# Three pairs of a scan's output products as seven block products among the next projections, decay factors on ScalarE

## Chip, cores and metric

One core of a Trainium2 chip runs the whole program. The metric is the device time of one execution in microseconds; of the kernel before three runs were timed: 2537.12 in the median, 2536.92 to 2539.6.

## What is computed

Two pre-norm layers on 256 tokens of width 2048: a Mamba-2 scan and an MLP, then dilated attention and an MLP, and a final norm. The change lies in the scan layer. Cut to what matters:

```python
zxbcdt = u @ w_in                      # z, xbc and dt side by side
xbc = silu(causal_depthwise_conv(xbc, conv_w, conv_b))
...
L = segsum_exp(a)                      # exp(cs[l] - cs[s]) for s <= l, else 0
cb = jnp.einsum("bclgn,bcsgn->bcgls", cm, bm)
y_diag = jnp.einsum("bcgls,bgjcls,bcsgjp->bclgjp", cb, L, x)
...
y = ssd_chunked(xs * dt[..., None], dt * A, bm, cm)
y = y + d_skip[:, None] * xs
y = y.reshape(Bsz, S, D_INNER) * silu(z)
yg = y.reshape(Bsz, S, SSM_GROUPS, D_INNER // SSM_GROUPS)
yg = yg * rsqrt(mean(yg * yg) + EPS)
x = x + (yg.reshape(Bsz, S, D_INNER) * norm_w) @ w_out
```

There are 8 groups of 512 channels (8 heads of 64), 2 chunks of 128 tokens, and a state of 128. All is float32.

## The kernel before, in words

**Matmuls.** Each float32 product is made of rounded parts: a weight is split into a high part `wh` (a ScalarE copy to fp32r, L232) and a low part `wl` (VectorE, the raw weight less `wh`, L233), the activation likewise, and TensorE adds high x high, high x low and low x high. A weight comes in units of 128x2048 (1 MB). `fetch` (L189 to L235) loads one (SyncE's queue, L216) into a raw buffer and splits it; `take` (L237) is called when a unit's matmuls are written down, and fetches every later unit of `plan` whose split buffer belongs to a unit already used. There are three pairs of split buffers (a fourth in the middle of the MLP), so the split of a unit may begin when the unit three places earlier has been multiplied.

**A group of the scan** (`group`, L514) has 10 units of `w_in`: six feature units c0 to c5 (`cols_units`, 16 matmuls of 512 columns and 16 of 256, L260), each followed by a convolution (`conv_tile`, L487: the two halves of a bank added, a scale, four taps, a silu), and four gate units z0 to z3 (`rows_unit`, 24 matmuls of 512 columns, L295 to L297). Then three parts follow, each written where an earlier group's generator is resumed:

- first part: the rows of cumulated decay come by DMA into `ab` (L560, one buffer, which the group before frees with its y matmuls); the product `cb` of the two state features (L574); 16 VectorE steps per group, `min(row - column, 0)` (L585); two Exp on ScalarE (L588); the product with `cb` (L590, "es"); transposes of the features (L597) and their scaled copies `xdt`, `xd`, `xdd`.
- second part: the state `st`, 64 small matmuls `y` (L623), the share of the earlier chunk `yo`, the gate, the norm.
- third part: transposes `yT` (L649) and the high and low parts `y3t` of the result (L655, L656).

**The output product** (`project`, L661) is written in blocks: after group 3 for groups 0 and 1, after group 5 for 2 and 3, after group 7 for 4 and 5, then 6, then 7. Each group has 4 units of `w_out`, one for each 512 columns of the result, 24 matmuls each; two results per unit are added into `x_res` (L302). With group 7 the norm of the next layer starts (`step_on`).

**What sets the order.** A scheduler orders all instructions by the order in which they are written and by their readiness; engines then run their queues strictly in that order and wait for each other by semaphores. `tc.issue_after(i)` keeps an instruction behind another. In the MLP the second product is already made from seven block products (Winograd's form of Strassen): `CHUNK_ORDER` writes feature units U and products in turn, TensorE's order is fixed, and the sums of weight blocks are made in a buffer A and a buffer B, partly by GpSimd's accumulating DMA (L218), which adds one more block onto a buffer after the split before has read it.

Of the kernel before, what the change touches and what calls it, by code (L numbers as in the profile page):

```python
# [14 lines left out]
P = 128  # L15
S = 256
# [28 lines left out]

def unit_plan():
    plan = []
    pairs = {3: (0, 1), 5: (2, 3)}
    for g in range(G):
        plan += [("in", g, u) for u in range(6)]  # L50
        if g == 0:
            plan.append(("dt",))
        plan += [("in", g, u) for u in range(6, 10)]
        if g in pairs:
            plan += [("out", gg, j) for j in range(4) for gg in pairs[g]]
    for gs in ((4, 5), (6,), (7,)):
        plan += [("out", gg, j) for j in range(4) for gg in gs]
# [17 lines left out]
}  # L75

# [16 lines left out]
def hybrid_trunk_kernel(ctx: ExitStack, tc: tile.TileContext, a: dict, out: bass.AP):  # L93
# [58 lines left out]
    def source(u):  # L152
# [32 lines left out]

    def split_slot(i):
        return splits.peek(range(4 if chunked(i) else 3))

    def fetch(i, ends=(16,)):  # L189

        src, n = source(plan[i])
        item = plan[i][3] if plan[i][0] == "w2" and len(plan[i]) == 4 else None
        where, _, _, how = PRODUCTS[item[0]] if item else ("raw", 0, 0, "load")
        if where == "raw":
            k = raws.use(raws.peek(range(2 if chunked(i) else 3)))
            raw = wts.tile([P, 2048], F32, tag=f"raw{k}", name=f"raw{i}", bufs=1)
        elif how == "load":
            if where + item[1] == "Aa":
                pool, tag = wts, f"raw{raws.use(2)}"
            else:  # L200
                pool, tag = mlp_pool[0], where + item[1]
            raw = pool.tile([P, 2048], F32, tag=tag, name=f"{where}{item[1]}{i}", bufs=1)
        else:
            raw = sums_of[where + item[1]]
        if where != "raw":
            sums_of[where + item[1]] = raw
# [6 lines left out]
        for k0, k1 in zip((0, *ends), ends):  # L213
# [3 lines left out]
            elif how == "add":  # L217
                nc.gpsimd.dma_start(raw[:, c], src[:, c], accum_op=ALU.add)  # L218
            with ExitStack() as order:
                if plan[i][0] in ("w1", "w2"):  # L220
# [151 lines left out]
    def ssm(nx):  # L372
# [9 lines left out]
        for j in range(4):  # L382
            n = KT if j == 0 else 0
            t = sp.tile([P, n + (8 if j else 4) * S], F32, tag="y3t", name=f"xt0_{j}", bufs=4)
            if j == 0:
                g0 = t[:, :KT]
            t_x = t[:, n:n + 4 * S].rearrange("p (q t) -> p q t", q=4)
            xt.append((t[:, n:n + 4 * S], t[:, 4 * S:] if j else None))
# [37 lines left out]
        def steps():  # L426
# [56 lines left out]
            sm.update(dt=dt, acs=acs, scratch=scratch, ddt=dec, eacs=eacs)  # L483

        y3 = {}

        def conv_tile(g, u, ps, tot=None):  # L487
# [12 lines left out]
            nc.scalar.activation(o, acc, AF.Silu, bias=cw[:, 4:5])  # L500
# [8 lines left out]
        def cross(ps, lhs, rhs):  # L509
            nc.tensor.matmul(ps, lhs[:, 0], rhs[:, 0], start=True, stop=False)  # L510
            nc.tensor.matmul(ps, lhs[:, 0], rhs[:, 1], start=False, stop=False)
            nc.tensor.matmul(ps, lhs[:, 1], rhs[:, 0], start=False, stop=True)

        def group(g, before):  # L514
# [3 lines left out]
            us, names = [("in", g, u) for u in range(6)], [f"c{g}_{u}" for u in range(6)]  # L518
            if g == 0:
# [17 lines left out]
            else:  # L537
                ch = []
                for u in range(6):
                    ch.append(conv_tile(g, u, cols_units([us[u]], xs, [names[u]], first=(u < 2))[0]))  # L540
                    if u == (4 if g == 1 else 2):
                        next(before, None)
            banks = [mm_bank(f"z{g}_{m}") for m in range(NH)]
            for q in range(4):
                rows_unit(banks, [("in", g, 6 + q)], lhs_x, 4 * q, 4, 512, q == 0, q == 3)
                if q == (3 if g == 1 else 1) and before is not None:
                    next(before, None)
            if g == 0:
                with tc.issue_after(load[12]):
                    for m in range(NH):  # L550
                        nc.sync.dma_start(x_res[:, m, :], a["x"][m * P:(m + 1) * P, :])
            zs = []
            for m in range(NH):
                z = sp.tile([P, GW], F32, tag="z", name=f"zs{g}_{m}", bufs=2)
                nc.scalar.activation(z, banks[m], AF.Silu, scale=n0.rs[:, m:m + 1])
                zs.append(z)

            ab = sp.tile([P, NH, HG, P], F32, tag="ab", name=f"ab{g}", bufs=1)
            rows = sm["scratch"][:, g * HG * P:(g + 1) * HG * P]
            nc.scalar.dma_start(ab.rearrange("p m h t -> p m (h t)"),  # L560
                                rows.unsqueeze(0).to_broadcast([P, NH, HG * P]))
            hs = slice(g * HG, (g + 1) * HG)
            bT, cT = ch[4], ch[5]

            def bc(v):
                return v.unsqueeze(2).to_broadcast([P, HG, HD])

            def heads(t):
                return t.rearrange("p (h d) -> p h d", h=HG)

            ps = sm_bank(f"cb{g}")
            for m in range(NH):
                t = slice(m * P, (m + 1) * P)
                nc.tensor.matmul(ps[:, t], bT[:, t], cT[:, t], start=(m == 0), stop=True,  # L574
                                 skip_group_check=True)
            cb = sp.tile([P, NH, P], F32, tag="cb", name=f"cbm{g}", bufs=1)
            nc.vector.tensor_tensor(cb, ps[:, :S].rearrange("p (m l) -> p m l", m=NH),
                                    tri[:, None, :].to_broadcast([P, NH, P]), ALU.mult)

            es = []  # L580
            for m in range(NH):
                e = ab[:, m]
                for h in range(HG):
                    av = sm["acs"][:, m, g * HG + h:g * HG + h + 1]
                    nc.vector.tensor_scalar(e[:, h], e[:, h], av, 0.0, ALU.subtract, ALU.min)  # L585
                es.append(e)
            for m in range(NH):
                nc.scalar.activation(es[m], es[m], AF.Exp)  # L588
            for m in range(NH):
                nc.vector.tensor_tensor(es[m], es[m], cb[:, m:m + 1, :].to_broadcast([P, HG, P]),  # L590
                                        ALU.mult)

            xdt, xd = [], []
            for m in range(NH):
                ps = sm_bank(f"xt{g}_{m}")
                for c in range(4):
                    nc.tensor.transpose(ps[:, c * P:(c + 1) * P], ch[c][:, m * P:(m + 1) * P], ident)  # L597
                t = sp.tile([P, GW], F32, tag="xdt", name=f"xdt{g}_{m}", bufs=2)
                nc.vector.tensor_tensor(heads(t), heads(ps), bc(sm["dt"][:, m, hs]), ALU.mult)
                xdt.append(t)  # L600
                t = sp.tile([P, GW], F32, tag="xd", name=f"xd{g}_{m}", bufs=2)
                nc.vector.tensor_tensor(heads(t), heads(ps), bc(dskip[:, hs]), ALU.mult)
                xd.append(t)
                if m == 0:
                    t = sp.tile([P, GW], F32, tag="yo", name=f"xdd{g}", bufs=1)
                    nc.vector.tensor_tensor(heads(t), heads(ps), bc(sm["ddt"][:, hs]), ALU.mult)
                    xdd = split(t, GW, "xdd", f"xdds{g}")
            ps = sm_bank(f"bt{g}")
            nc.tensor.transpose(ps[:, :P], bT[:, :P], ident)
            btok = split(ps[:, :P], P, "bs", f"btok{g}")  # L610
            cs = split(cT[:, P:], P, "bs", f"cs{g}")
            yield

            ps = sm_bank(f"st{g}")
            cross(ps, btok, xdd)
            state = split(ps, GW, "xdd", f"state{g}")
            ys = []
            for m in range(NH):
                ps = sm_bank(f"y{g}_{m}")
                for h in range(HG):  # L620
                    for c in range(2):
                        l = slice(c * 64, (c + 1) * 64)
                        nc.tensor.matmul(ps[l, h * HD:(h + 1) * HD], es[m][:, h, l],  # L623
                                         xdt[m][:, h * HD:(h + 1) * HD], start=(h == 0), stop=True,
                                         skip_group_check=True)
                y = xd[m]
# [498 lines left out]
```

## Time and profile before

| | |
|---|---|
| profiled execution | 2538.28 us |
| its span, first to last instruction | 2536.4 us |
| median of three timed runs | 2537.12 us |
| granted TensorE clock | 0.999 |
| busy in the span: TensorE, VectorE, ScalarE, GpSimd | 100%, 80%, 60%, 4% |
| first matmul of the first MLP | 686.65 us |
| matmuls of the scan's output product | 768, of 512 columns |
| read from HBM | 544.16 MB |

A row of a view has line, engine, operation, output and inputs by their names in the program, sizes and a count. In the grouped view, behind the bar, stand the busy time, the mean of one in ns, and the idle time of the engine just before, with what ended it. In the chain and in the timeline a row begins with its start in us from the span's start and its length. The lengths of TensorE and VectorE instructions overlap with the next ones, so the time that one takes in a queue is the distance of two starts.

### The profile page before, as it was taken

Reading aid. Unit: us, or ns where it says so; the run is one execution under the profiler, and the core shown is the slowest. Engines: PE = TensorE matmul, PEld = TensorE weight load, DVE = VectorE, ACT = ScalarE, POOL = GpSimd, SP = SyncE. Lnnn points to the kernel's source line nnn. Section 1 sums busy time; section 2 is a strip of 40 time slices with the busy share of each in tenths; the row PEclk is TensorE's granted clock in tenths of the full one; section 3 lists DMA queues with packets and bytes.
Section 4 is the critical chain, followed back from the end, with each engine's and each line's share of the span. In section 5 each row is a group of like instructions: output and inputs, shape, how many; then the busy total and the mean of one; then the engine's idle time right before and its main releaser. Section 6 shows DMA issues by size and latency. Waiting matters only on the chain.

```text
span 2536.4 us, 34422 instructions
## 1 busy us (share of the span) xinstructions
PE 2523.8 (100%) x13809; PEld 2175.5 (86%) x13809; DVE 2021.8 (80%) x2370; ACT 1532.3 (60%) x1826; POOL 101.0 (4%) x119
## 2 busy tenths in 40 slices
PE   9999999999999999999999999999999999999998
PEld 7888888888888888888888999999888888888887
DVE  7888687687678889888886667767668998889885
ACT  7676466564566666566555656666566666666664
POOL 0000000000000000000000000000000000000001
PEclk9999999999999999999999999999999999999999
DMA  7655555555688898889955545444568988898884
GB/s 283 222 183 194 186 186 193 190 184 183 217 226 247 254 252 260 256 251 254 261 193 175 174 174 169 165 162 163 173 223 231 265 251 252 247 269 252 254 234 143
DMA packets 81105, 548.57 MB, mean 216 GB/s; under 512 B 9008, under 2 KB 9648, under 8 KB 19760
## 3 DMA queue, kind: packets, MB, share of 16 engines
q1 hardware_dynamic: 66096, 447.79, 49.6%
q0 software_dynamic: 12096, 88.09, 17.7%
q10 hardware_dynamic: 2752, 10.49, 1.3%
q8 instruction: 109, 1.79, 0.3%
q14 instruction: 52, 0.43, 0.0%
HBM read 544.16 MB, written 2.16 MB: 215 GB/s over the span
## 4 chain that ended last, share of the span: by engine, by line
PE 98%; DMA 1%; DVE 0%; issue 0%; ACT 0%; SPq 0%; ACTq 0%; POOLq 0%; POOL 0%; DVEq 0%
PE h L260 28%; PE qk L260 11%; PE c L260 10%; PE pxb L938 6%; PE pxa L938 6%; PE pwb L938 3%; PE pwa L938 3%; PE wo L296 2%; PE wo L295 2%; PE z L296 2%; PE z L297 2%; PE z L295 2%; PE wo L297 2%; PE v L297 2%; PE v L295 2%; PE v L296 2%
## 5 line engine op out<-in xcount | busy, mean ns | idle before, releaser
L233 DVE TENSOR_TENSOR wl<-raw,wh 128x2048 fp32r<-128x2048 f32 (+4 forms) x386 | 837.6, 2172 | 336.1 <-ACT wh L232 335.0
L232 ACT ACTIVATE wh<-raw 128x2048 fp32r<-128x2048 f32 (+4 forms) x386 | 704.1, 1826 | 450.5 <-PE wo L297 84.0
L260 PE MATMUL h<-xn,wh 128*128 128x512 f32 x2048 | 690.0, 393 | 0.0
L260 PE MATMUL h<-xn,wl 128*128 128x256 f32 x2048 | 555.5, 280 | 0.0
L260 PEld LDWEIGHTS h<-xn,wh 128*128 128x128 f32 x2048 | 376.4, 188 | 75.8
L260 PEld LDWEIGHTS h<-xn,wl 128*128 128x128 f32 x2048 | 385.0, 188 | 13.8
L260 PE MATMUL c<-xn,wh 128*128 128x512 f32 x768 | 267.5, 395 | 2.2 <-ACT wh L232 2.2
L260 PE MATMUL qk<-xn,wh 128*128 128x512 f32 x768 | 259.3, 393 | 0.0
L260 PE MATMUL c<-xn,wl 128*128 128x256 f32 x768 | 212.4, 282 | 0.8 <-DVE wl L233 0.8
L260 PE MATMUL qk<-xn,wl 128*128 128x256 f32 x768 | 209.2, 283 | 0.0
L260 PEld LDWEIGHTS c<-xn,wh 128*128 128x128 f32 x768 | 143.1, 188 | 35.0 <-ACT wh L232 4.5
L260 PEld LDWEIGHTS qk<-xn,wh 128*128 128x128 f32 x768 | 141.1, 188 | 28.8
L260 PEld LDWEIGHTS c<-xn,wl 128*128 128x128 f32 x768 | 143.7, 188 | 3.6 <-DVE wl L233 1.4
L260 PEld LDWEIGHTS qk<-xn,wl 128*128 128x128 f32 x768 | 141.4, 188 | 3.6 <-issue 1.2
L232 ACT ACTIVATE wh<-Ab 128x2048 fp32r<-128x2048 f32 x42 | 80.4, 1915 | 78.5 <-DMA Ab<-in_w 59.3
L233 DVE TENSOR_TENSOR wl<-Ab,wh 128x2048 fp32r<-128x2048 f32 x42 | 96.0, 2287 | 18.0 <-ACT wh L232 18.0
L232 ACT ACTIVATE wh<-Aa 128x2048 fp32r<-128x2048 f32 x42 | 80.3, 1912 | 40.4 <-DMA Aa<-in_w 33.3
L233 DVE TENSOR_TENSOR wl<-Aa,wh 128x2048 fp32r<-128x2048 f32 x42 | 96.0, 2286 | 9.8 <-ACT wh L232 9.8
L297 PE MATMUL z<-wh,xn 128*128 128x512 f32 x256 | 100.3, 392 | 0.0
L295 PE MATMUL wo<-wh,y3t 128*128 128x512 f32 x256 | 100.2, 393 | 0.0
L296 PE MATMUL wo<-wl,y3t 128*128 128x512 f32 x256 | 100.0, 391 | 0.0
L295 PE MATMUL z<-wh,xn 128*128 128x512 f32 x256 | 100.0, 391 | 0.0
(372 smaller groups left out, 4776.0 us busy)
## 6 DMA issues: line engine op xcount, KB each, us to landing
raw<-in_w SPq DMA_DIRECT2D x172, 1024.0 KB, 5.4
raw<-in_w_in SPq DMA_DIRECT2D x74, 1024.0 KB, 4.9
raw<-in_w_qk SPq DMA_DIRECT2D x48, 1024.0 KB, 4.8
raw<-in_w_out SPq DMA_DIRECT2D x32, 1024.0 KB, 4.8
Aa<-in_w POOLq DMA_DIRECT2D x28, 1024.0 KB, 10.1
Ab<-in_w POOLq DMA_DIRECT2D x28, 1024.0 KB, 10.1
raw<-in_w_v SPq DMA_DIRECT2D x32, 768.0 KB, 4.3
Ab<-in_w SPq DMA_DIRECT2D x14, 1024.0 KB, 4.8
```

The costliest lines, as they stand in the source:

```text
L232: high[i] = nc.scalar.activation(wh[:, c], raw[:, c], AF.Copy).ins
L233: low[i] = nc.vector.tensor_tensor(wl[:, c], raw[:, c], wh[:, c].bitcast(F32), ALU.subtract).ins
L260: latest[0] = nc.tensor.matmul(ps[:, :n], (wh, wl)[part][:, kt * P:(kt + 1) * P], xs[:, kt, :, :].rearrange("p a t -> p (a t)")[:, :n], st ...
L295: nc.tensor.matmul(banks[m][:, :n], hi, wh[:, c], start=st, stop=False)
L296: nc.tensor.matmul(banks[m][:, :n], hi, wl[:, c], start=False, stop=False)
L297: latest[0] = nc.tensor.matmul(banks[m][:, :n], lo, wh[:, c], start=False, stop=sp).ins
L938: latest[0] = nc.tensor.matmul(ps, lhs(i, part), w[:, n], start=(first and i == 0 and part == 0 and w is wh), stop=(i == 3 and part == 1), ...
```

## The change

`GROUP_ORDER` now writes, for each group from 1 on, what is put down in which order: c0 to c5 and z0 to z3 of this group, `y` and `Y` (second part of the group before, in two halves), `t` (its third part), `f` (first part of this group), `p` (operands of a pair), digits (products of the pair in work), `oGJ` (unit J of group G, as before). From group 3 on TensorE's order is fixed to it. The pairs are groups 0 and 1, 2 and 3, 4 and 5; a pair's products for the first half of the columns lie in one group (3, 5, 7), for the second half in the next (4, 6, and the tail 8). Groups 6 and 7 keep plain units, in the tail. Each product has 12 matmuls of 512 columns.

The weight sums of a half are made on buffer A (1: load, 5, 6, 4: one block more added each time) and B (3: load, 7: one more added), all additions by GpSimd's DMA; 2 is a plain load. Two raw buffers are left beside A. The operands of a pair, four sums and seven splits, are 11 steps on VectorE and 7 on ScalarE, put down at `p`. Each product is added into `x_res` by a VectorE step (14 per pair, where 8 were).

The decay factors become `exp(-|row - column|)`: 16 Abs per group on ScalarE with the negated column as bias, then two Exp with scale -1, kept behind the last silus; the upper triangle is masked by `cb` as before.

```diff
+GROUP_ORDER = {
...
+    **{g: "c0 c1 1 c2 y c3 Y 5 c4 3 c5 t 6 z0 7 f z1 2 z2 4 z3" + " p" * (g % 2 == 0) for g in range(3, 7)},
...
+    8: "1 o60 y o61 Y 5 o62 3 o63 t 6 7 o70 2 o71 4 o72 o73",
+}
...
+PUT = {"1": ("x", 0, 0, ALU.add), "6": ("x", 0, 1, ALU.subtract), "7": ("x", 1, 1, ALU.add),
+       "4": ("x", 1, 0, ALU.subtract), "5": ("w", 1, 1, ALU.add), "3": ("w", 0, 1, ALU.subtract),
+       "2": ("z", 0, 0, ALU.add)}
...
+        if kind == "wq":
+            where, _, _, how = PRODUCTS[plan[i][2]]
...
-            k = raws.use(raws.peek(range(2 if chunked(i) else 3)))
+            k = raws.use(raws.peek(range(2 if few(i) else 3)))
...
-            elif how == "add":
+            elif how == "add" or kind == "wq":
                 nc.gpsimd.dma_start(raw[:, c], src[:, c], accum_op=ALU.add)
             with ExitStack() as order:
-                if plan[i][0] in ("w1", "w2"):
+                if kind in ("w1", "w2") or few(i):
                     order.enter_context(tc.issue_after(high[i - 1]))
                     order.enter_context(tc.issue_after(low[i - 1]))
...
+        def put_in_order(make):
+            if not fixed[0]:
+                return make()
+            with tc.issue_after(latest[0]):
+                return make()
...
-                for h in range(HG):
-                    av = sm["acs"][:, m, g * HG + h:g * HG + h + 1]
-                    nc.vector.tensor_scalar(e[:, h], e[:, h], av, 0.0, ALU.subtract, ALU.min)
...
+                    for h in range(HG):
+                        av = sm["less"][:, m, g * HG + h:g * HG + h + 1]
+                        nc.scalar.activation(es[m][:, h], es[m][:, h], AF.Abs, bias=av)
...
+        def product(pair, item, half):
+            key, m, j, op = PUT[item]
...
+                wh, wl = take("wq", pair, item, half)
+                lhs = of[pair][item]
+                for i in range(4):
+                    n = slice(i * 512, (i + 1) * 512)
+                    for part, w in ((0, wh), (0, wl), (1, wh)):
+                        latest[0] = nc.tensor.matmul(
+                            ps, lhs[:, i, part], w[:, n],
...
+            xc = x_res[:, m, j * 512:(j + 1) * 512]
+            nc.vector.tensor_tensor(xc, xc, ps, op)
...
+        def operands(pair):
...
+            parts("1", a11)
+            parts("4", a22)
+            nc.vector.tensor_tensor(a22, a21, a22, ALU.subtract)
+            parts("5", a22)
+            nc.vector.tensor_tensor(a21, a11, a21, ALU.add)
+            nc.vector.scalar_tensor_tensor(a11, a22, -1.0, a11, op0=ALU.mult, op1=ALU.subtract)
+            parts("2", a12)
+            nc.vector.scalar_tensor_tensor(a12, a12, -1.0, a11, op0=ALU.mult, op1=ALU.subtract)
+            parts("3", a12)
+            parts("6", a11)
+            parts("7", a21)
```

**ScalarE in group 4, after the y matmuls of group 3.** Before, from the DMA of the decay rows on (`ab4`) the queue had a tap of the convolution and the next unit's high part:

```order
L560 DMA ab4_3294<-acs_rows_600 128x2x1024
L636 ACTIVATE ssq_junk_75,sq3_0_2956<-xd3_0_2497 128x512
L495 ACTIVATE c4_2a_2923<-upad0_188,vecs_176 128x256
L232 ACTIVATE wh55_3048<-raw55_3047 128x2048
L278 ACTIVATE c4_3x_3035<-c4_3_3002 128x256
```

Now 13 of the 16 Abs on `ab4` (L643) stand between that DMA and the high part `wh55`, which belongs to product 3 (buffer B):

```order
L620 DMA ab4_3183<-acs_rows_603 128x2x1024
L710 ACTIVATE ssq_junk_75,sq3_0_2885<-xd3_0_2514 128x512
L643 ACTIVATE ab4_3183<-ab4_3183,acs_598 128x128 x4
L533 ACTIVATE c4_2a_2835<-upad0_191,vecs_179 128x256
L643 ACTIVATE ab4_3183<-ab4_3183,acs_598 128x128 x9
L313 ACTIVATE c4_3x_2932<-c4_3_2893 128x256
L538 ACTIVATE c4_1o_2770<-c4_1a_2765,vecs_179 128x256
L713 ACTIVATE xd3_0_2514<-xd3_0_2514,rq3_0_2887 128x512
L267 ACTIVATE wh55_2961<-B55_2960 128x2048
```

So the Abs, which need the decay rows, are ahead of that split.

**VectorE in group 4, at the evacuation of c5** (`c4_5t`). Before, it stood behind the low part of a plain unit:

```order
L233 TENSOR_TENSOR wl57_3153<-raw57_3151,wh57_3152 128x2048
L281 TENSOR_TENSOR c4_5t_3139<-c4_5_3104,c4_5x_3137 128x256
L307 TENSOR_SCALAR rt3_1_2992<-sq3_1_2989 128x1
L497 SCALAR_TENSOR_TENSOR c4_4a_3091<-upad0_188,vecs_176,c4_4a_3091 128x256
L492 TENSOR_TENSOR upad1_190<-c4_5t_3139,xn0rb_363 128x256
```

Now it stands behind `wl59`, the low part for product 7, whose buffer B (`B55`, loaded for product 3) has to receive GpSimd's addition first:

```order
L268 TENSOR_TENSOR wl57_3031<-A50_2671,wh57_3030 128x2048
L316 TENSOR_TENSOR c4_4t_3020<-c4_4_2979,c4_4x_3018 128x256
L535 SCALAR_TENSOR_TENSOR c4_3a_2937<-upad1_193,vecs_179,c4_3a_2937 128x256
L268 TENSOR_TENSOR wl58_3051<-raw58_3049,wh58_3050 128x2048
L530 TENSOR_TENSOR upad0_191<-c4_4t_3020,xn0rb_366 128x256
L268 TENSOR_TENSOR wl59_3115<-B55_2960,wh59_3114 128x2048
L316 TENSOR_TENSOR c4_5t_3089<-c4_5_3048,c4_5x_3087 128x256
L793 TENSOR_TENSOR x_res_69<-x_res_69,qx0b_2772 128x512
```

So everything from the evacuation of c5 on is queued behind that addition.

**VectorE in group 4, ahead of product 4.** Now the last rows up to its low part `wl63` are these; `cbm4` and `xdt4_0` stand just ahead of them, behind `wl62`, and `op1_3` and L764 are operand steps of the next pair:

```order
L662 TENSOR_TENSOR xd4_0_3217<-xt4_0_3210,vecs_179 128x512
L666 TENSOR_TENSOR xdd4_3219<-xt4_0_3210,dec_607 128x512
L764 SCALAR_TENSOR_TENSOR yT3_3099<-yT3_3099,yT2_2396 128x4x128
L659 TENSOR_TENSOR xdt4_1_3229<-xt4_1_3224,dta_594 128x512
L662 TENSOR_TENSOR xd4_1_3231<-xt4_1_3224,vecs_179 128x512
L544 TENSOR_TENSOR btok4_3235<-bt4_3233,btok4_3235 128x128
L544 TENSOR_TENSOR cs4_3238<-c4_5o_3097,cs4_3238 128x128
L650 TENSOR_TENSOR ab4_3183<-ab4_3183,cbm4_3188 128x1024 x2
L544 TENSOR_TENSOR xdds4_3221<-xdd4_3219,xdds4_3221 128x512
L755 TENSOR_TENSOR op1_3_3375<-yT3_3099,op1_3_3375 128x4x128
L263 SCALAR_TENSOR_TENSOR wl63_3273<-A50_2671,wh63_3272 128x2048
```

Before, the first part of group 4 stood after the last gate unit of its group and ahead of the splits of the next units, `wl61` and `wl62`:

```order
L590 TENSOR_TENSOR ab4_3294<-ab4_3294,cbm4_3299 128x1024 x2
L602 TENSOR_TENSOR xd4_0_3328<-xt4_0_3321,vecs_176 128x512
L606 TENSOR_TENSOR xdd4_3330<-xt4_0_3321,dec_604 128x512
L599 TENSOR_TENSOR xdt4_1_3340<-xt4_1_3335,dta_591 128x512
L602 TENSOR_TENSOR xd4_1_3342<-xt4_1_3335,vecs_176 128x512
L233 TENSOR_TENSOR wl61_3354<-raw61_3352,wh61_3353 128x2048
```

So this burst has moved in among the gate units and products, with operand steps added to it.

More of the change, by code (lines that the diff above doesn't have):

```diff
@@ L184, in chunked, with few @@
         return plan[i][0] == "w1" and plan[i][2] > 0 or plan[i][0] == "w2" and len(plan[i]) == 4
+    quads = [i for i, u in enumerate(plan) if u[0] == "wq"]
+    def few(i):
+        return chunked(i) or quads[0] <= i and plan[i][0] in ("in", "out", "wq")
     def split_slot(i):
@@ L509, in cross, with small, __init__, begin @@
         def cross(ps, lhs, rhs):
[L510 to L519, printed above, removed]
+            small(lambda: [nc.tensor.matmul(ps, lhs[:, a], rhs[:, b], start=a + b == 0, stop=a == 1)
+                           for a, b in ((0, 0), (0, 1), (1, 0))])
+        fixed = [False]
+        def put_in_order(make):
[3 more added lines that the diff above has]
+                return make()
+        def small(make):
+            latest[0] = put_in_order(make)[-1].ins
+        class Group:
+            def __init__(self, g):
+                self.g, self.ch, self.banks = g, [], None
+            def begin(self):
+                g = 0
+                us, names = [("in", g, u) for u in range(6)], [f"c{g}_{u}" for u in range(6)]
                 made = cols_units(us[:3], xs, names[:3], (1, 4, 8, 12), between=lambda: warm(1))
@@ L536, in group @@
                 steps()
[L537 to L547, printed above, removed]
@@ L572, in group @@
[L572 to L580, printed above, removed]
@@ L593, in group @@
[L593 to L607, printed above, removed]
@@ L659, in group @@
-            y3[g] = y3t
-        def project(gs, nxt=None, before=None):
-            for j in range(4):
-                banks = [mm_bank(f"wo{gs[0]}_{j}_{m}") for m in range(NH)]
-                for g in gs:
-                    lhs = lambda k, part, t, g=g: y3[g][:, k, part, t]
-                    rows_unit(banks, [("out", g, j)], lhs, 0, 4, 512, g == gs[0], g == gs[-1])
-                add_residual(banks, j)
-                step_on(nxt, j)
-                if before is not None and j in (0, 3):
-                    next(before, None)
@@ L672, in ssm, with features @@
[L672 to L683 removed]
+                self.ch = ch
+            def features(self, u):
+                g, name = self.g, f"c{self.g}_{u}"
+                unit = lambda made=None: cols_units([("in", g, u)], xs, [name], first=(u != 1 if g >= 3 else u < 2),
+                                                     made=made)[0]
+                ps = put_in_order(lambda: unit([bank(name, (0, 1))] if g >= 3 else None))
+                self.ch.append(conv_tile(g, u, ps))
@@ new lines, in ssm, with matmuls @@
+        of, sums7 = {}, {}
+        def product(pair, item, half):
+            key, m, j, op = PUT[item]
+            if item in "152":
+                name = f"q{key}{pair}{half}"
+                sums7[key] = sm_bank(name) if key == "z" else bank(name, (2,) if key == "x" else (3,))
+            ps = sums7[key]
+            def matmuls():
+                wh, wl = take("wq", pair, item, half)
[5 more added lines that the diff above has]
+                            ps, lhs[:, i, part], w[:, n],
+                            start=(item in "152" and i == 0 and part == 0 and w is wh),
+                            stop=(i == 3 and part == 1), skip_group_check=True).ins
+            put_in_order(matmuls)
+            j += 2 * (half == "b")
+            xc = x_res[:, m, j * 512:(j + 1) * 512]
+            nc.vector.tensor_tensor(xc, xc, ps, op)
@@ new lines, in plain @@
+        def plain(g, j):
+            banks = [bank(f"wo{g}_{j}_{m}", (0, 1)) for m in range(NH)]
+            lhs = lambda k, part, t: y3[g][t.start // P][:, k, part]
+            put_in_order(lambda: rows_unit(banks, [("out", g, j)], lhs, 0, 4, 512, True, True))
+            add_residual(banks, j)
+            if g == 7:
+                step_on(nx, j)
+        cur = Group(0)
+        cur.begin()
+        for q in range(4):
+            cur.gate(q)
+        with tc.issue_after(load[12]):
+            for m in range(NH):
+                nc.sync.dma_start(x_res[:, m, :], a["x"][m * P:(m + 1) * P, :])
@@ new lines, in ssm @@
+        cur.first()
+        for g, order in GROUP_ORDER.items():
+            before = cur
+            cur = Group(g)
+            fixed[0] = g >= 3
+            for item in order:
+                if item[0] == "c":
+                    cur.features(int(item[1]))
+                elif item[0] == "z":
+                    cur.gate(int(item[1]))
+                elif item == "y":
+                    rest = before.second()
+                    next(rest)
+                elif item == "Y":
+                    next(rest, None)
+                elif item == "t":
+                    before.third()
+                elif item == "f":
+                    cur.first()
+                elif item == "p":
+                    of[(g - 2) // 2] = operands((g - 2) // 2)
+                elif item[0] == "o":
+                    plain(int(item[1]), int(item[2]))
+                else:
+                    product((g - 3) // 2, item, "ab"[(g - 3) % 2])
@@ L962, in mlp @@
                     continue
-                key, m, j, op = put[item[0]]
+                key, m, j, op = PUT[item[0]]
                 key += item[1]
```

280 lines of the change are left out of this document (168 added, 112 removed).

## Prediction

> **What bounds the kernel now.** I read the split of the profile page first, then the busy table by stage, then TensorE's order in time.
>
> ```profile
> PE 2523.8 (100%) x13809; PEld 2175.5 (86%) x13809; DVE 2021.8 (80%) x2370; ACT 1532.3 (60%) x1826; POOL 101.0 (4%) x119
> PE 98%; DMA 1%; DVE 0%; issue 0%; ACT 0%; SPq 0%; ACTq 0%; POOLq 0%; POOL 0%; DVEq 0%
> 198.00:364.40 166.40, 166.40 (x953) 141.38 (x952) 124.18 (x177) 95.41 (x109) 2.86 (x4) 1.00 0.56 190
> 900.00:1400.00 500.00, 500.00 (x2580) 428.48 (x2579) 423.70 (x414) 305.79 (x330) 26.13 (x30) 1.00 0.79 237
> ```
>
> The chain that ended last is TensorE for 98%. The third row is two scan groups with the output product of a pair between them (columns: length; busy PE, PEld, DVE, ACT, POOL; clock, DMA share, GB/s): TensorE never rests, VectorE is busy for 75%. The fourth is the MLP, where the seven-product scheme already stands: VectorE 85%, TensorE still without a gap. "Busy" covers overlapped matmuls, so I take paces from start to start:
>
> ```profile
> 263.09 0.39 PE L297 MATMUL wo<-wh,y3t 128*128 128x512 f32 x1
> 265.81 0.39 PE L297 MATMUL wo<-wh,y3t 128*128 128x512 f32 x1
> 364.44 16.72 PE c L260 x96
> 732.22 2.73 PE pxa L938 x12
> ```
>
> Twelve matmuls of 512 columns take 2.72 us, 0.227 each, and the MLP's seven-scheme products run at the same pace (2.73). A z or output unit (24) is 5.44, a feature unit (c) 16.72/3 = 5.57, a product 2.72.
>
> **What is removed.** A pair had 8 units x 24 = 192 output matmuls, and has 14 products x 12 = 168. Three pairs lose 72: 72 x 0.227 = **16.3 us**, all on the path, since TensorE sets the end throughout. The Trainium skill, "TensorE: Matmul & The Clock Gate", section "Back-to-back issue gap", gives a sustained 131 ns at 512 columns; by that the 72 would be worth 9.4 us. The two rows above decide for 0.227 and I give that figure no chance.
>
> **VectorE and ScalarE in sum.** Start-to-start times come from these rows (VectorE, then ScalarE):
>
> ```profile
> 366.81 0.68 DVE L602 TENSOR_TENSOR xd<-xt,vecs 128x512 f32<-128x512 f32 x1
> 367.41 0.68 DVE L606 TENSOR_TENSOR xdd<-xt,dec 128x512 f32<-128x512 f32 x1
> 369.21 2.28 DVE L233 TENSOR_TENSOR wl<-raw,wh 128x2048 fp32r<-128x2048 f32 x1
> 371.41 0.28 DVE L506 TENSOR_TENSOR btok<-bt,btok 128x128 fp32r<-128x128 f32 x1
> 371.61 0.28 DVE L506 TENSOR_TENSOR cs<-c_5o,cs 128x128 fp32r<-128x128 f32 x1
> 379.75 0.42 DVE L281 TENSOR_TENSOR c_1t<-c,c_1x 128x256 f32<-128x256 f32 x1
> 380.08 0.48 DVE L497 SCALAR_TENSOR_TENSOR c_0a<-upad,vecs,c_0a 128x256 f32<-128x256 f32 x1
> 380.47 0.42 DVE L492 TENSOR_TENSOR upad<-c_1t,xn0rb 128x256 f32<-128x256 f32 x1
> 390.00 2.05 DVE L585 TENSOR_SCALAR ab<-ab,acs 128x128 f32<-128x128 f32 x10 [0.76 <-DMA ab<-acs_rows]
> 416.54 0.87 DVE L656 SCALAR_TENSOR_TENSOR y3t<-yT,vecs,y3t 128x256 fp32r<-128x256 f32 x2
> 402.95 0.51 ACT L500 ACTIVATE c_2o<-c_2a,vecs 128x256 f32<-128x256 f32 x1
> 403.37 1.91 ACT L232 ACTIVATE wh<-raw 128x2048 fp32r<-128x2048 f32 x1
> 405.18 0.36 ACT L278 ACTIVATE c_5x<-c 128x256 f32<-128x256 f32 x1
> 405.44 0.62 ACT L636 ACTIVATE ssq_junk<-xd 128x512 f32<-128x512 f32 x1
> ...
> 406.06 0.49 ACT L495 ACTIVATE c_4a<-upad,vecs 128x256 f32<-128x256 f32 x1
> 406.46 0.49 ACT L500 ACTIVATE c_3o<-c_3a,vecs 128x256 f32<-128x256 f32 x1
> ```
>
> VectorE: 2.20 for a weight's low part (wl), 0.60 for 512 columns, 0.33 for 256 (0.39 with a third operand), 0.20 for 128. ScalarE: 1.81 for a high part (wh), 0.42 for a silu, 0.26 for a copy of 256 columns, 0.40 for one with a scale per partition (406.06), 0.6 for 512. Over two groups VectorE loses 32 decay steps x 0.2 = 6.4 and 8 low parts of y x 0.44 = 3.5, and gains 6 weight splits (13.2), 11 operand steps (6.6) and 6 residual adds (3.6): 124.2 + 13.5 = 138 in 160 us of TensorE, 86%, the MLP's share. On totals it holds. What can fail is one item: an item needs its wh and wl, and with three buffers its split may begin only when the item three places earlier has ended. Two items were 11 us of cover and are now one unit and one product, 8.2.
>
> **The chain inside a group.** I count from the end of the scan's y matmuls (item y); the order rows of the change give the queue.
>
> ```profile
> 383.92 0.37 ACTq L560 DMA_DIRECT2D ab<-acs_rows  x1
> 759.74 0.30 ACT L889 ACTIVATE a<-r 128x128 fp32r<-128x128 f32 x1
> 759.94 1.92 ACT L232 ACTIVATE wh<-raw 128x2048 fp32r<-128x2048 f32 x1
> 363.02 0.44 PE cb L574 x4
> 363.46 0.87 PE xt L597 x8
> 185.00 0.87 PE yT L649 x8
> 387.10 0.23 PE yo L510
> ```
>
> The decay rows ab are fetched into the one buffer that y has just freed: issued at 383.92, used at 390.00, so 6.1 us. Then ScalarE does 13 Abs ahead of product 3's high part. No row has Abs: at least 0.20 each (the copy at 759.74), at most 0.34 (that plus the 0.14 that 0.40 stands above 0.26); I take 0.27, nearer to the copy, as shape and engine are its own: 3.5. Four short steps (0.40, 0.26, 0.42, 0.6) and wh make it 13.1, wl 15.4. TensorE comes there at c3 5.57 + yo 0.69 (three of 0.23) + product 5 2.72 + c4 5.57 = 14.55; the first matmul (0.2) needs wh alone, so product 3 waits **0.7** (0 to 1.6 by the two ends).
>
> Product 3's wl lets GpSimd add the next block onto the same buffer, for product 7. What such a transfer takes is seen in the MLP alone (GpSimd's issues in order of time; then microseconds to landing of the issues at 749.58, 753.25 and 811.11; then the medians):
>
> ```profile
> 749.58 0.87 POOL L218 DMA_DIRECT2D Ab<-in_w  x1 [8.22 <-DVE wl L233]
> 753.25 0.87 POOL L218 DMA_DIRECT2D Ba<-in_w  x1 [2.80 <-DVE wl L233]
> 811.11 0.88 POOL L218 DMA_DIRECT2D Aa<-in_w  x1 [48.66 <-DVE wl L233]
> ...
> Ab<-in_w POOLq DMA_DIRECT2D x1, 1024.0 KB, 10.6
> ...
> Ba<-in_w POOLq DMA_DIRECT2D x1, 1024.0 KB, 14.0
> ...
> Aa<-in_w POOLq DMA_DIRECT2D x1, 1024.0 KB, 8.7
> ...
> Aa<-in_w POOLq DMA_DIRECT2D x28, 1024.0 KB, 10.1
> Ba<-in_w POOLq DMA_DIRECT2D x14, 1024.0 KB, 12.5
> ```
>
> The one that follows another by 3.7 us takes 14.0, the one after a long pause 8.7. In the new order the addition for product 7 follows the last one by about 16 us, so I take **8.7**, and keep 12.5 as the far end. It lands at 24.4 (0.3 to issue); wh 26.2, wl 28.5. Behind this wl on VectorE stands c5's evacuation (28.8), whose bank the second half of z0 needs at 14.55 + 0.7 + 2.72 + 5.57 + 0.87 + 2.72 + 2.72 = 29.85: 1 us spare.
>
> After product 7's wl the second half of a pair has 33 rows on VectorE up to product 4's wl: 4 wl (8.8), 16 of 0.60 (9.6), 6 of 0.39 and 3 of 0.33 (3.3), 2 of 0.20 (0.4), and two es products of 1024 columns (2.3, an estimate between 0.60 and 2.20): 24.4, ending at 52.9. TensorE is there at 27.1 + z0 5.44 + 7 2.72 + f 1.42 + z1 5.44 + 2 2.72 + z2 5.44 = 50.3, so it is **2.4 late** (2.6 less a matmul). A transfer that took no time would still leave over 1 us of it, as wl 7 then waits for its buffer. The first half has no operand steps; its z2 split ends 3 wl (6.6), 7 of 0.60, 6 of 0.39, 3 of 0.33 and the es pair after product 7's, 16.4 in all, at 44.9, and is needed at 44.85: nothing.
>
> First halves (groups 3, 5, 7) so lose 0.7 each and second halves (4, 6) 3.1: 2.1 + 6.2 = 8.3. The tail adds 2: the low parts of y for group 7 stand on VectorE behind one 2.20 split when the first o7 unit begins (0 to 3). Groups 1 and 2 keep 11 us of cover and lose nothing (0 to 1).
>
> The rest is hidden. 18 MB more are read, under products that leave DMA lighter than in the MLP (0.56 to 0.79 above). The 24 new additions have GpSimd's queue almost to themselves (2.86 us busy of 166), and 6 loads less pass SP. Table loads fall, off the path.
>
> Sum: 16.3 - 8.3 - 2.0 = 6.0 us gained. The profiled execution took 2538.28 with a span of 2536.4, 1.2 above the median of 2537.12; against the median this is **2531 us**.
>
> **Rivals.**
>
> *Even (2537.7).* The additions land at the median of 10.1. Then c5's evacuation is 0.4 late, first halves lose 1.95, second halves 4.5, in all 16.9 with the tail: +0.6. For it: 10.1 is what 28 issues show. Against it: those are closer together.
>
> *Slower (2550).* The addition for product 7 collides with weight loads and the addition for product 4, which is issued some 5 us later, and lands after 12.5, as Ba does. Then z0 waits 2.8 in every group, first halves lose 4.35, second halves 6.9, with the tail 28.9: +12.6. Each microsecond of landing costs about 5 in all; it decides from 11.0 on (+5). The Trainium skill, "SBUF — State Buffer", names a mechanism for it, the "DVE blocks DMA" trap: GpSimd cannot write descriptors while VectorE holds the shared port. GpSimd's 0.87 above, with VectorE 85% busy, shows no sign of it.
>
> *Fully covered (2522).* VectorE's queue runs ahead where I have it waiting, as in the MLP, whose DMA waits reach ScalarE but not TensorE. Only a few microseconds are lost: 16.3 - 1.5 = 14.8. Against it: the 24.4 us of rows behind product 7's wl stand in that order, whatever the transfer takes.
>
> ```profile
> L232 ACT ACTIVATE wh<-Ab 128x2048 fp32r<-128x2048 f32 x42 | 80.4, 1915 | 78.5 <-DMA Ab<-in_w 59.3 <-DVE wl L233 12.6 <-PE h L260 5.5
> ```
>
> That the change does not save matmuls can be left out: they are counted in the order.
>
> **How the numbers follow.** My forecast 0.40 (2526 to 2537 by its own bounds), even 0.23, slower 0.20, covered 0.17. About 0.2% (5.1 us) is what a measurement of this kernel can tell from no change. Faster by more than that: the covered case and 0.28 of the forecast's 0.40, 0.45. Within: 0.12 and the even case, 0.35. Slower: 0.20. The range reaches from the covered case at 2521 to a landing of about 11.8 us, 2546; the worst of the slow case stays outside.
>
> **What would show it.** Right: TensorE's groups show 72 fewer output matmuls; in groups 4 and 6 TensorE waits on wl ahead of product 4 by about 2 us and in all five ahead of product 3 by under 1; additions to B land in 8.5 to 9.5 us. Wrong: waits of z on c5's evacuation (landing was longer), no waits at all in 200 to 640 us, or a loss in the MLP or attention, which the change does not touch.

## The result, and the profile after

| | before | after |
|---|---|---|
| median of the timed runs | 2537.02 us (2536.57 to 2539.6) | 2601.44 us (2599.93 to 2602.75) |
| span of the profiled execution | 2536.4 us | 2601.0 us |
| granted TensorE clock | 0.999 | 0.985 |

The ratio is 1.0252, with a 95% interval of 1.0234 to 1.0269: slower by 64.4 us, where 6 us of gain were forecast. The first lines of the page after, and the split of the chain that ended last:

```profile
span 2601.0 us, 34411 instructions
PE 2532.7 (97%) x13737; PEld 2176.2 (84%) x13737; DVE 2058.6 (79%) x2296; ACT 1602.2 (62%) x1991; POOL 119.8 (5%) x143
...
PE 77%; DMA 2%; ACT 1%; DVE 1%; issue 0%; ACTq 0%; POOLq 0%; POOL 0%
```

The 72 matmuls are gone (13809 before, 13737 now). The 77% of TensorE cannot be set beside the 98% of before: this chain could be followed back only to 456.4 us of the span, the one before to its first microseconds. The busy table by stage, in stretches of 48 to 100 us (a group takes about 95 us here; length; busy PE, PEld, DVE, ACT, POOL; clock, DMA share, GB/s), says where the time goes:

```profile
200.00:248.00 48.00, 40.92 (x265) 34.76 (x264) 32.34 (x42) 25.58 (x43) 3.94 (x5) 0.93 0.59 168
...
332.00:412.00 80.00, 70.23 (x385) 58.92 (x386) 61.61 (x67) 52.20 (x59) 4.24 (x5) 0.91 0.67 201
...
490.00:575.00 85.00, 74.78 (x407) 62.45 (x407) 66.75 (x81) 54.59 (x76) 4.11 (x5) 0.92 0.65 201
575.00:660.00 85.00, 71.09 (x395) 59.04 (x394) 57.44 (x76) 46.83 (x69) 4.97 (x6) 0.88 0.63 186
...
sum 645.00, PE 589.13 PEld 492.46 DVE 482.71 ACT 407.30 POOL 31.79; mean PE 73.64 PEld 61.56 DVE 60.34 ACT 50.91 POOL 3.97
```

No engine is full here. TensorE, which had no gap before in this stretch, stands 645 - 589.1 = 55.9 us between 100 and 745 us, and its clock is lowest in the rows in which it stands most. Since 64.4 = 55.9 of idle - 16.3 saved + 24.8, the 24.8 us are what is left over, and I put them down to work at a lower clock. The clocks of all eight stretches allow it: 1 less the clock, times the length, adds up to 34.4 us, the time included in which TensorE stood. What TensorE waits for, between 200 and 660 us (in all, times, longest):

```profile
PE cb L633 <- ACT c_5o L538: 17.7, 3, 6.2
PE qw0a L785 <- DVE x_res L793: 5.7, 1, 5.7
PE qw0b L785 <- ACT wh L267: 3.5, 1, 3.5
PE qw2a L785 <- ACT wh L267: 3.4, 1, 3.4
PE qw1b L785 <- ACT wh L267: 3.0, 1, 3.0
PE qw1a L785 <- ACT wh L267: 2.5, 1, 2.5
...
PE qw1a L785 <- DVE wl L268: 1.7, 1, 1.7
```

There are two places. Product 3 (the second on bank `qw`) waits in every group: for its high part, then 1.5 to 1.7 for its low part; in group 3 for the add of product 5, which is queued behind that low part. And `cb`, the first matmuls of the item f, waits for the silu of c5 in groups 4, 6 and 7. No z waits for the evacuation of c5. The chain of waits in group 6 passes through both:

```profile
501.36 10.25 DMA ab<-acs_rows
...
513.23 1.31 ACT ab L643 x5
...
517.24 1.81 ACT wh L267
...
519.07 2.30 DVE wl L268
...
521.66 9.69 DMA B<-in_w_out
...
533.39 2.29 DVE wl L268
535.68 0.34 DVE c_5t L316
...
537.74 2.21 DVE wl L268
...
539.97 6.56 DMA raw<-in_w_in
...
546.61 1.91 ACT wh L267
548.52 0.41 ACT c_5o L538
...
548.97 1.22 PE cb L633 x4
```

The decay rows take 10.25 us, the Abs stand ahead of product 3's high part, its low part releases the addition to B, and that one holds c5's evacuation. Then c5's silu, whose last tap is done by 545.5, stands on ScalarE behind the high part of another unit, whose load could start only when the low part at 537.74 had left its raw buffer. TensorE had reached `cb` at 543.3.

GpSimd's addition 5 to 6 is issued at 497.98, 3.4 us ahead of the decay rows. The DMA issues between 200 and 660 us (times, KB, median us to landing):

```profile
raw<-in_w_in SPq DMA_DIRECT2D x46, 1024.0 KB, 4.9
A<-in_w_out POOLq DMA_DIRECT2D x15, 1024.0 KB, 9.0
raw<-in_w_out SPq DMA_DIRECT2D x6, 1024.0 KB, 8.0
...
ab<-acs_rows ACTq DMA_DIRECT2D x5, 1024.0 KB, 10.6
B<-in_w_out POOLq DMA_DIRECT2D x5, 1024.0 KB, 8.7
```

The additions land as forecast (8.7). The decay rows, at 6.1 before, do not. The kernel after itself shows both times: 6.0 to 6.6 us in groups 0 to 2, where nothing is added yet, and 9.8 to 12.3 us in groups 3 to 7. After a wait TensorE works slowly for a while; product 3 of group 6 in order of time:

```profile
519.09 0.79 PE L785 MATMUL qw1b<-wh,op 128*128 128x512 f32 x1 [3.05 <-ACT wh L267]
521.42 0.80 PE L785 MATMUL qw1b<-wl,op 128*128 128x512 f32 x1 [1.53 <-DVE wl L268]
...
522.87 0.63 PE L785 MATMUL qw1b<-wl,op 128*128 128x512 f32 x1
523.29 1.06 PE L785 MATMUL qw1b<-wh,op 128*128 128x512 f32 x2
524.14 0.63 PE L785 MATMUL qw1b<-wl,op 128*128 128x512 f32 x1
```

Three matmuls take 1.27 us (522.87 to 524.14), 0.42 each against 0.227. The Trainium skill, "TensorE: Matmul & The Clock Gate", section "HAM oscillation — how this bites in real kernels", says that a pause of over some 3.4 us lets the next work start at half rate. The pitch agrees (0.42 is 1.9 times 0.227), the length of the wait only roughly: the first matmul behind the wait of 3.05 us has a length of 0.79 where 0.39 is usual, while in e6_vector_decays the matmuls behind a wait of 3.88 us (at 325.8 us) run on at 0.23.

### The profile page after: what moved, and what is told of

Same layout as the page of the kernel before. It is cut to its first block, busy times and chain, and to the rows that moved or that the text cites. A ratio compares the mean times of both kernels' runs of the same rounds, so it can differ in the third digit from the quotient of the medians.

```text
span 2601.0 us, 34411 instructions
## 1 busy us (share of the span) xinstructions
PE 2532.7 (97%) x13737; PEld 2176.2 (84%) x13737; DVE 2058.6 (79%) x2296; ACT 1602.2 (62%) x1991; POOL 119.8 (5%) x143
## 4 chain that ended last, share of the span: by engine, by line
PE 77%; DMA 2%; ACT 1%; DVE 1%; issue 0%; ACTq 0%; POOLq 0%; POOL 0%
PE h L295 27%; PE qk L295 10%; PE pxb L1089 6%; PE pxa L1089 6%; PE pwb L1089 3%; PE pwa L1089 3%; PE v L330 2%; PE v L331 2%; PE v L332 2%; PE c L295 2%; PE pzb L1089 1%; PE pza L1089 1%; PE d L330 1%; PE d L331 1%; PE d L332 1%; PE s L860 1%
## 5 line engine op out<-in xcount | busy, mean ns | idle before, releaser
L268 DVE TENSOR_TENSOR wl<-raw,wh 128x2048 fp32r<-128x2048 f32 (+4 forms) x368 | 796.7, 2167 | 299.4 <-ACT wh L267 298.2
L267 ACT ACTIVATE wh<-raw 128x2048 fp32r<-128x2048 f32 (+4 forms) x368 | 669.8, 1822 | 397.9 <-PE h L295 80.8
L295 PEld LDWEIGHTS c<-xn,wh 128*128 128x128 f32 x768 | 142.2, 188 | 31.8 <-ACT wh L267 2.6
L295 PEld LDWEIGHTS qk<-xn,wh 128*128 128x128 f32 x768 | 141.1, 188 | 28.8
L295 PEld LDWEIGHTS c<-xn,wl 128*128 128x128 f32 x768 | 144.0, 188 | 10.6 <-DVE wl L268 3.5
L331 PE MATMUL z<-wl,xn 128*128 128x512 f32 x256 | 101.0, 394 | 0.0
L1038 ACT ACTIVATE r<-r 128x256 f32<-128x256 f32 x128 | 52.2, 411 | 73.0 <-DVE r L1037 73.0
```

The source lines that it names most:

```text
L267: high[i] = nc.scalar.activation(wh[:, c], raw[:, c], AF.Copy).ins
L268: low[i] = nc.vector.tensor_tensor(wl[:, c], raw[:, c], wh[:, c].bitcast(F32), ALU.subtract).ins
L295: latest[0] = nc.tensor.matmul(ps[:, :n], (wh, wl)[part][:, kt * P:(kt + 1) * P], xs[:, kt, :, :].rearrange("p a t -> p (a t)")[:, :n], st ...
L331: nc.tensor.matmul(banks[m][:, :n], hi, wl[:, c], start=False, stop=False)
L1038: nc.scalar.activation(t, t, AF.Square)
```

## The experiments

All groups from 3 on are meant unless another is named. A time without a ratio is that of one execution, and is compared with 2601.44 us of the kernel after.

**The Abs behind other high parts** (e1_abs_late).

```diff
+                        with ExitStack() as order:
+                            if g >= 3:
+                                order.enter_context(tc.issue_after(high[cursor[1] - 4 + (m * HG + h) // 4]))
+                            nc.scalar.activation(es[m][:, h], es[m][:, h], AF.Abs, bias=av)
```

> The one edit: in groups 3 to 7 the 16 Abs are spread, four behind each of the last four high parts written down when the first part is, so that none stands ahead of product 3's high part. Queue theory (the losses are in-order waits: decay rows late, Abs queued ahead of product 3's high part; c5's silu queued behind another unit's split): the 24 us of TensorE waits ahead of product 3 go to under 5, with about half of the 34 us that the lower clock costs; the 17.7 us ahead of cb stay: 2555 to 2570. Traffic theory (the accumulating transfers keep the weights late): product 3's high part then waits for buffer B or a raw load, little is gained: 2590 to 2601. Fixed-order theory: the wait moves to another place in the same group: 2590 or more.

Measured: 2559.27 us, 42 less, in the queue theory's range. The waits between 200 and 660 us:

```profile
PE cb L633 <- ACT c_5o L538: 12.4, 5, 4.7
PE bt L672 <- DVE y3t L745: 7.4, 1, 7.4
```

The second is in group 7, where f waits for the low parts of group 6's y. Not one is ahead of product 3, though the decay rows still land in 10.7 us. What cost there was the place of the Abs in ScalarE's queue; the slow transfers alone, with nothing urgent behind them, cost nothing there.

**The first part later** (e2_f_late), groups 3 to 7.

```diff
-c0 c1 1 c2 y c3 Y 5 c4 3 c5 t 6 z0 7 f z1 2 z2 4 z3
+c0 c1 1 c2 y c3 Y 5 c4 3 c5 t 6 z0 7 z1 2 z2 f 4 z3
```

> The one edit: in groups 3 to 7 the first part f stands behind z2 instead of behind product 7, 13.6 us of TensorE later. Queue theory: the 17.7 us of waits ahead of cb go, with about half of the clock's 34; those ahead of product 3 stay at about 24: 2562 to 2575. Traffic theory: the raw load that c5's silu stands behind is late for the units themselves, so the wait turns up at z2 or at product 4: 2590 or more.

Measured: 2582.27 us, 19 less, where at least 26 were expected. The waits ahead of `cb` are gone, those ahead of product 3 are as they were (25.9 us in all, 24.3 in the kernel after), and the waits of feature units for their low parts rose from 1.6 to 4.3 us.

**Both** (e3_both): the two diffs together.

> Both edits together. Queue theory: nearly all waits in groups 3 to 7 and the low clock go, and the 16.3 us of saved matmuls show, less a few us of low parts that come late ahead of product 4 and in the tail: 2522 to 2535, clock 0.995 or more. Traffic theory: 2570 or more, with TensorE waiting for low parts whose buffers land late.

Measured: 2537.86 us, ratio to before 1.0002 (0.9992 to 1.0012), above the range of the queue theory by 3 us. The two edits add up (42.2 + 19.2 = 61.4; together 63.6). The loss is located, but the saving does not show. Between 200 and 660 us these waits remain:

```profile
PE qx2b L788 <- DVE x_res L796: 3.4, 1, 3.4
PE yo L548 <- DVE state L544: 1.3, 1, 1.3
PE c L295 <- ACT zs L613: 1.3, 1, 1.3
PE c L295 <- DVE cs L544: 0.5, 2, 0.3
```

Another 2.5 us lie in group 1, ahead of y; the clock stands at 0.98 in that stretch.

**Plain loads in place of the additions** (e4_plain_loads).

```diff
-            elif how == "add" or kind == "wq":
+            elif kind == "wq":
+                nc.gpsimd.dma_start(raw[:, c], src[:, c])
+            elif how == "add":
                 nc.gpsimd.dma_start(raw[:, c], src[:, c], accum_op=ALU.add)
```

> The kernel after with GpSimd's additions in the scan made plain loads on the same queue (the block replaces the sum: the sums of weight blocks are left out), everything else in its place. Queue theory: the transfers get shorter, the decay rows land a few us sooner, but the Abs still stand ahead of product 3's high part and c5's silu behind its split: 2570 to 2595. Traffic theory: the waits go with the accumulation: 2525 to 2545.

Measured: 2568.52 us, 33 less, 1.5 us under the queue theory's range and far from that of the traffic theory. Landing, between 200 and 660 us, and then the waits:

```profile
A<-in_w_out POOLq DMA_DIRECT2D x17, 1024.0 KB, 5.2
raw<-in_w_out SPq DMA_DIRECT2D x10, 1024.0 KB, 5.3
...
ab<-acs_rows ACTq DMA_DIRECT2D x5, 1024.0 KB, 6.2
```

```profile
PE cb L635 <- ACT c_5o L540: 16.0, 3, 6.6
...
PE qw1a L787 <- DVE wl L270: 1.1, 1, 1.1
...
PE qw0b L787 <- DVE wl L270: 0.6, 1, 0.6
```

This tells the causes apart. That the weights are added rather than loaded is what slows the decay rows from 6.2 to 10.6 us and a plain load of `w_out` from 5.3 to 8.0. By what mechanism an addition does that, no run shows. With 6.2, product 3 waits 0.6 to 1.1 in four groups and not at all in group 3, as the prediction had it. The waits ahead of `cb` hardly change (17.7 us before this edit), so they do not hang on the additions, and e2 showed that they go with the place of f.

**The decays on VectorE again** (e6_vector_decays).

```diff
-                        nc.scalar.activation(es[m][:, h], es[m][:, h], AF.Abs, bias=av)
+                        nc.vector.tensor_scalar(es[m][:, h], es[m][:, h], av, 0.0, ALU.add, ALU.min)
```

> The kernel after with the decay factors on VectorE again (16 subtract-and-min steps per group, Exp as before). In the new order these steps now stand on VectorE ahead of product 3's low part and wait there for the same decay rows, while c5's silu gets ahead of two more splits on ScalarE. Queue theory: the wait ahead of product 3 shrinks by about 3 us in each group but stays (1 to 2 us, for the low part), the one ahead of cb falls to under 3: 2545 to 2572. Theory that the decays on ScalarE are the whole loss: 2520 to 2537.

Measured: 2591.35 us, outside both ranges. The waits ahead of `cb` are gone, as expected; those between 200 and 660 us are now these:

```profile
PE yT L728 <- ACT xd L713: 15.3, 5, 3.1
...
PE qw1b L785 <- DVE x_res L793: 4.2, 1, 4.2
...
PE qw1a L785 <- DVE x_res L793: 3.7, 1, 3.7
```

The wait has changed engines: now the decay steps hold up VectorE's queue (19.9 us in four waits for the decay rows), and the add of product 5 and the norm's steps stand behind them. I had counted the low part and not these. The decays on ScalarE are not the loss; a step that needs late data, put ahead of urgent work on either engine, is.

**Matmuls that nothing needs** (e7_filler): `fill(bank, 16)` ahead of product 3, `fill(bank, 20)` ahead of `cb` in groups 4, 6 and 7.

```diff
+        def fill(ps, n):
+            small(lambda: [nc.tensor.matmul(ps, xs[:, 0, 0, :P], xs[:, 0, :, :].rearrange("p a t -> p (a t)"),
+                                            start=True, stop=True, skip_group_check=True) for _ in range(n)])
```

> The kernel after with matmuls that nothing needs: 16 of 512 columns (3.6 us) ahead of each product 3 in groups 3 to 7, 20 (4.5 us) ahead of cb in groups 4, 6 and 7, so that TensorE works where it waited. The waits that end are the same. If the low clock follows from the waits: clock 0.994 or more and 2570 to 2585, the difference to 2601 being the clock's part. If the clock has another cause: clock about 0.985 and 2600 or more.

Measured: 2598.46 us at a clock of 0.995; the clock rose as expected, the time did not follow. The sum over 100 to 745 us:

```profile
sum 645.00, PE 613.17 PEld 512.40 DVE 488.72 ACT 408.90 POOL 31.70; mean PE 76.65 PEld 64.05 DVE 61.09 ACT 51.11 POOL 3.96
```

Idle is 31.8 us, the fillers another 140 x 0.227 = 31.8: 63.6 us without use, where 55.9 were idle before. So the low clock does follow from the waits, but this run wins back only 3.0 us of the 24.8. A reading that fits is that a faster TensorE comes sooner to the next wait, whose end the other queues set: the waits of feature units for the gate's silu (`zs`) rose from 2.5 to 8.7 us. How much of the 7.7 us more is that, and how much a filler running past the end of a wait, this run does not show.

**The order of TensorE left to the scheduler** (e10_free_order).

```diff
-            fixed[0] = g >= 3
```

> The kernel after with TensorE's order left to the scheduler also from group 3 on (nothing else edited; the other queues follow from the same rules). Fixed-order theory (the loss is that TensorE may not do later work while it waits): most of it comes back, 2535 to 2555. Queue theory: the scheduler does not know the waits either, and the Abs and the silu of c5 stand where they stood: 2570 to 2605.

Measured: 2575.4 us, 26 less, in the queue theory's range, though the run is not as clean as it was meant: the decay rows are now fetched at other times. ScalarE's rows for them in groups 3 and 4:

```profile
227.10 0.37 ACTq L620 DMA_DIRECT2D ab<-acs_rows  x1
240.09 3.32 ACT L643 ACTIVATE ab<-ab,acs 128x128 f32<-128x128 f32 x11 [5.54 <-DMA ab<-acs_rows]
287.63 0.37 ACTq L620 DMA_DIRECT2D ab<-acs_rows  x1
293.37 1.28 ACT L643 ACTIVATE ab<-ab,acs 128x128 f32<-128x128 f32 x4 [4.05 <-DMA ab<-acs_rows]
```

In group 3 GpSimd had issued an addition at 225.47, 1.6 us before, and the rows took 13.0 us; in group 4 the last addition was at 252.94 and the next came at 307.98, and they took 5.7. In groups 5 to 7 no addition had been issued just before either, and they took 5.8 to 6.4. So in one kernel, with the same instructions, an addition issued just before goes with the long time and none with the short. How much of the 26 us comes from this and how much from pieces of later units that fill waits stays open; 38 us remain in any case.

**The decays alone, in the old order** (e8_before_abs), and the same with the Abs held behind two high parts (e11_before_abs_late, the three lines ahead of the Abs).

```diff
-                    nc.vector.tensor_scalar(e[:, h], e[:, h], av, 0.0, ALU.subtract, ALU.min)
+                    with ExitStack() as order:
+                        if g >= 1:
+                            order.enter_context(tc.issue_after(high[cursor[1] - 2 + (m * HG + h) // 8]))
+                        nc.scalar.activation(e[:, h], e[:, h], AF.Abs, bias=av)
```

> The kernel before with one part of the change alone: the 16 decay steps of a group as Abs on ScalarE with the negated column, Exp with scale -1. Its output product, its loads and its order are as before, so a split has 11 us of cover and the decay rows land in 6 us. Queue theory: within 0.3 %, 2533 to 2544. Theory that the decays on ScalarE are the whole loss: 2560 or more.

> The kernel of e8_before_abs (the old order and output product, decays as Abs on ScalarE) with the Abs of groups 1 to 7 held behind the last two high parts written when the first part is, eight behind each. Queue theory: the 12 us that the Abs cost in the old order come from steps behind them on ScalarE (the scaled copy xd that the transposes yT wait for, 5.8 us in 6 waits), so they go but for group 1: 2536 to 2542. If ScalarE's added 4.8 us per group are themselves the cost: 2546 to 2552.

Measured: 2549.30 us (ratio 1.0047, 1.0033 to 1.0061) and 2541.19 us (1.0016, 1.0007 to 1.0025). The first lies between the two expectations: the Abs cost 12 us even where a split has 11 us of cover. TensorE waits, from 100 to 700 us, in the first:

```profile
PE yT L650 <- ACT xd L640: 5.8, 6, 1.8
PE y L624 <- DVE ab L591: 2.2, 1, 2.2
```

The second is in its range. Held back, the Abs leave the wait of y in group 1 (2.5) and 0.8 us at `cb`. So 8 of the 12 us were again what stood behind them; 4 us remain.

**Two more places** (e5_two_more) **and three more** (e9_three_more). The orders of e9 against those of e3_both (e5 has its group 1, and in the tail `3 o63 t 6 2 7`); in e9 groups 3 to 6 change as 7 does, and group 0's decays are on VectorE besides.

```diff
-    1: "c0 c1 c2 c3 c4 y Y c5 z0 z1 z2 z3 t f",
+    1: "c0 c1 c2 c3 c4 c5 y Y z0 z1 z2 z3 t f",
-    7: "c0 c1 1 c2 y c3 Y 5 c4 3 c5 t 6 z0 7 z1 2 z2 f 4 z3",
-    8: "1 o60 y o61 Y 5 o62 3 o63 t 6 7 o70 2 o71 4 o72 o73",
+    7: "c0 c1 1 c2 y c3 Y 5 c4 3 c5 t 6 z0 7 z1 2 z2 f z3 4",
+    8: "1 o60 y o61 Y 5 o62 3 t o63 6 2 7 o70 o71 4 o72 o73",
```

> The kernel of e3_both with two more places moved: in group 1 the items y and Y stand behind c5 instead of behind c4 (there TensorE waited 2.5 us for the first decays and lost 2 us to the clock), and in the tail the order is 6 2 7 instead of 6 7 (there product 7 waited 3.4 us for the add of product 6 and lost 3.3 us to the clock). Queue theory: about 11 us of what was left of the 16.3 come back, 2524 to 2531 with the ratio's interval below 1. Rival, that the saving itself is smaller than the counted 72 matmuls (a pace that the trace does not show): no faster than e3_both, 2535 to 2540.

> The kernel of e5_two_more with three more places mended: group 0's decays on VectorE as before (in group 1 TensorE still waited 2.5 us for them, and ran 2 us at the low clock), z3 ahead of product 4 (so that c0 of the next group does not wait for the gate's silu, 2.3 us in three waits), and in the tail t behind product 3 instead of behind o63 (the units of group 7 waited 3.6 us for their operands). Queue theory: about 8 us less than e5_two_more, 2524 to 2531, the ratio's interval wholly below 0.999. Rival, that VectorE and ScalarE are full and a wait that is moved comes back elsewhere: 2533 to 2538.

Measured: 2535.62 us (ratio 0.9989, 0.9980 to 0.9998), above its range: y in group 1 still waited 2.5 us for the decays (in e9, with group 0's on VectorE, that wait is gone), and the tail's wait had moved to the units of group 7. Then 2530.35 us (0.9970, 0.9959 to 0.9982), in its range. The sum of e9 over 100 to 745 us:

```profile
sum 645.00, PE 635.66 PEld 538.46 DVE 536.88 ACT 441.95 POOL 36.56; mean PE 79.46 PEld 67.31 DVE 67.11 ACT 55.24 POOL 4.57
```

Idle is 9.3 us, the clock 0.999: 9.3 - 16.3 = -7.0. The spans of the two profiled executions differ by 2530.2 - 2536.4 = -6.2, the medians by 2530.35 - 2537.23 = -6.9. So the 16.3 us are real to about 1 us, and this version is faster than the kernel before by 0.2 to 0.4%.

## Why the prediction was wrong, step by step

Two steps of the chain inside a group failed: what product 3 waits for, where the landing of the decay rows was taken from a quieter program, and the silu of c5, which f needs and for which nothing was charged.

- *72 matmuls at 0.227, 16.3 us*: right. Two groups took 166.40 us before (the prediction's third row) and take 160.90 in e9 (362.30 to 523.20), TensorE busy for 160.82 of them: 5.5 us less for 24 matmuls, and 24 x 0.227 is 5.45. At the 131 ns of the Trainium skill ("TensorE: Matmul & The Clock Gate", section "Back-to-back issue gap") it would have been 3.1. The totals held too: VectorE is busy for 138.1 us of that stretch, where 138 in 160 were forecast.
- *Product 3 waits 0.7*: here the prediction failed first, and by more: 0.7 in each of five groups is 3.5 us, and 24.3 were measured. The chain was right, one row in it was not. "Issued at 383.92, used at 390.00, so 6.1 us" was read in a program that adds nothing by DMA in the scan; the change puts an addition 3.4 us ahead of those rows, and they took 10.25. The Abs took 0.30 each, not 0.27. With these two figures the prediction's own sum puts the high part at 17.6 instead of 13.1, 3.1 us behind TensorE, and in group 6 product 3 waited 3.05 us for it and 1.53 for its low part. I weighed the additions for their own landing, and left out what they do to a transfer that the change does not touch. e4 gives the step back: at 6.2 it is 0.6 to 1.1, or nothing.
- *Additions to B in 8.7, z0 not late*: right, and the rival that was to end slower did not happen. That rival got the sign, but by another mechanism, and its 2550 is 51 us short. GpSimd's issues still took 0.86 to 0.90, one of them 1.04, so the "DVE blocks DMA" trap (the Trainium skill, "SBUF — State Buffer", section "SBUF: two separate sides") shows no sign here either.
- *c5's evacuation has 1 us spare*: z0 indeed did not wait, but here the prediction failed a second time. It followed the bank that the evacuation frees, not the result. f was put at 27.1 + 5.44 + 2.72 = 35.3 of that count, 6.5 us behind the evacuation at 28.8, and nothing was charged. In group 6 the evacuation begins at 535.60 and the silu ends at 548.9: 13.3 us through operand steps, two low parts, and a high part that waits for its load. That is 17.7 us of waiting in three groups, and e2 wins 19 by the place of f alone.
- *Product 4 is 2.4 late in groups 4 and 6*: no such wait is in any run, and it was not tested by itself. In group 6 of the kernel after its low part was done 26.3 us behind that of product 7 (535.68 to 562.02), near the 24.4 forecast, but TensorE, held up for 5.6 us by `cb`, came only at 565.8.
- *The tail loses 2*: the size is luck. The first o7 unit starts without a wait (719.29). Just ahead of it product 7 waits 2.3 us, put down to y3t; the add of product 6, on whose bank it goes on, also ended only then (714.87). Two waits of group 7's f on the low parts of group 6's y, 2.8 us in all, stood in no term.
- *Nothing for the clock*: by sums it was 24.8, though in e7 only 3.0 came back with the clock alone. The prediction had no term for it.
- *The range*: its lower end, 2521, lies 1 us under the covered case's own 2522. Nothing hangs on it.

## What to carry to other kernels

Where engines run their queues in order, an engine with time to spare does not make a step free: follow each result to its reader through every queue that it passes, and look for a step that needs late data ahead of one that others wait for. A duration from a trace holds for the traffic of that trace, so a change that adds transfers puts every other transfer on the path in question, not only its own. With the decays and the first part put where nothing urgent follows, and five more places moved, the same idea was worth 6.9 us (e9).

## What the runs showed of the hardware

- Between 200 and 660 us a transfer of 1 MB on GpSimd's queue landed in 5.2 to 5.3 us as a load (e4) and in 8.7 to 9.0 as an addition (the kernel after), in the median.
- The broadcast of the decay rows, 1 MB on ScalarE's queue, took 9.8 to 13.0 us each of the 40 times that an addition had been issued 1 to 4 us before it (nine kernels). Where no transfer of GpSimd's had been issued just before, it took 5.3 to 7.7 us in 58 of 59 cases; the other, in group 2 of e9, took 10.4, so other traffic can slow it too.
- Behind a wait of 3.05 us TensorE ran matmuls of 512 columns at 0.42 us instead of 0.227 (the kernel after), behind one of 3.88 us at 0.23 (e6).
- An Abs of 128x128 on ScalarE took 0.30 us, half again as long as the 0.20 of VectorE's step on the same block.
